# A two-layer decoder trunk: the order of TensorE's work around and inside the first layer's attention

## The chip, the cores and the metric

The kernel runs on one core of a Trainium2 chip. The core has TensorE (PE) for matrix products, VectorE (DVE), ScalarE (ACT) and GpSimd (POOL) for the rest, and SyncE (SP), which here only issues transfers. Each engine works through its own instructions in the order in which the program lists them, and semaphores hold it back until what it needs is there. The metric is the time of one execution on the device, in microseconds.

## The reference

Two layers on 512 positions of width 1024, each a token mixer and a feed-forward part, with a residual sum and a layer norm behind both. The change touches the mixer of the first layer, which is sixteen attention heads and an output projection:

```python
def even_mixer(x, w_in, w_uk, w_uv, b_f, w_o, rel_bias):
    h = x @ w_in
    q_a, c_kv, q_idx, k_idx, w_idx, q_b, k_b, v_b, f_in = _split(h, EVEN_WIDTHS)
    ...
    def block(args):                       # 128 queries at a time
        idx = jnp.einsum('bthd,bsd->bths', qi, k_idx)
        score = jnp.einsum('bth,bths->bts', wi, jax.nn.relu(idx)).astype(jnp.float32)
        score = jnp.where(causal[None], score, -jnp.inf)
        _, sel = lax.top_k(score, k_sel)   # 128 keys for each query
        ...
        la = jnp.einsum('bthr,btkr->bhtk', ql, c_sel).astype(jnp.float32)
        bias = rel_bias[t5_bucket(q_pos[None, :, None] - sel)]
        la = la + jnp.moveaxis(bias, -1, 1).astype(jnp.float32)
        ...
        oa = jnp.einsum('bhtk,btkr->bthr', pa, c_sel)
        lb = jnp.einsum('bthd,bshd->bhts', qb, k_b).astype(jnp.float32)
        lb = lb + jnp.swapaxes(fq, 1, 2)[..., None] - cum_f_keys[:, :, None, :]
        ...
        ob = jnp.einsum('bhts,bshd->bthd', pb, v_b)
    ...
    return jnp.concatenate([o_a, o_b], axis=-1) @ w_o
```

Eight heads "b" (first in the kernel, 0 to 7) attend with a forget bias to all earlier positions; eight heads "a" (8 to 15) attend to the 128 keys that the indexer's scores select, with a relative-position bias.

## The kernel before

Every large product is made from numbers split in two parts, high and low, and takes three products on TensorE: high by high, high by low and low by high (`mm3`, L175 to L177). A weight matrix comes by a transfer into `raw`, ScalarE casts its high part (L77), and VectorE, for some units GpSimd, makes the low part by subtraction (L81, L79). Units of the stream of weights are numbered in the order in which the program asks for them; units 10 to 17 are the projections of the "b" heads' pairs, 18 to 22 those of the "a" heads, 23 to 30 the output projection's.

The first layer's mixer runs in this order: the projections of the indexer's keys, the forget gates and the indexer's queries, the projection of c_kv; then the relative bias table (L418 to L437): a one-hot matrix and `rel_bias` are fetched, two small products (L422, L428) make the table, it is written to memory (`tb_d`), spread to one copy for each of 128 rows (`tp_d`), and read back shifted (`T5`), all transfers issued by GpSimd; then four transposes (L441) and the indexer's scores for the query blocks 1 to 3 (L457: for each of 8 indexer heads two products of 256, 384 or 512 columns; relu on ScalarE, L459; weighted sum on VectorE into `sel`, L462 and L464; masking on GpSimd, L466); then the values' projection of the "b" heads, and the projections of the first two pairs of heads.

After that the attention loop runs. For a head h it has four steps, which a string of letters, `SEQ`, orders: L makes the logits (for four query blocks 128, 256, 384 and 512 columns, three products each, over 64 rows of the array, into three banks); S is the softmax (VectorE adds the bias and takes the row's minimum, L616; ScalarE the exponential, L618); T transposes the weights, ten 128x128 blocks into one tile `tri` of three banks (L636), which ScalarE and VectorE then split into `pt` (L213, L214); V multiplies with the values (512, 384, 256 and 128 columns). B sets up the next head's bias, D divides by the sums, and a digit runs that many steps of `todo`, a generator of the projections that later heads need: filler for TensorE. One round does L of head h, T of head h-1 and V of head h-2:

```python
SEQ = "L2BT2SDV2"
```

The order on each engine isn't the source's: a scheduler simulates the program and places each instruction when it thinks that it can run. After the loop comes the output projection `out_ln`, its eight accumulators in eight banks, then the layer norm.

TensorE's results go to PSUM, which has eight banks. The kernel sets up three pools one after another: eight single banks up to the loop, five single ones and `tri` in the loop, eight single ones after it. A new pool opens a bank when the old pool's tiles in it are done with.

## Time and profile before

| | us |
|---|---|
| median of 3 runs | 1187.08 |
| lowest and highest run | 1183.45, 1188.37 |
| the profiled execution | 1182.65 |
| its span | 1180.9 |
| TensorE busy in it | 1158.8 |
| VectorE, ScalarE, GpSimd busy | 690.8, 465.5, 186.5 |

The profile is of one execution. Its span is the time from the first to the last instruction, and 1.75 us of the execution lie around it. A row of the time line has the start, the time for which the row was busy, the engine, the source line, the operation, what it writes and reads, and its shape; behind it, in brackets, the idle time of the engine just before and what ended it. Products are pipelined, so their recorded lengths overlap; what a product costs in a row is the distance of two starts.

### The profile page before, as it was taken

The page shows a single profiled execution, that of the slowest core. Times are in us where ns is not written, and L with a number is a line of the kernel's source. Part 1 is how long each engine was busy: PE and PEld are TensorE (multiplying, and loading weights), DVE is VectorE, ACT ScalarE, POOL GpSimd, SP SyncE. Part 2 cuts the span into 40 slices and gives each one's busy share as a digit, 9 for nine tenths or more (in the row PEclk, how much of TensorE's full clock was granted, in tenths as well). Part 3 has the DMA queues.
Part 4 walks back from the last instruction along what each step waited for, and adds up shares of the span by engine and source line. Part 5 has one row for each costly group of instructions (what it writes and reads, how often), then busy time and mean ns, then how long its engine had stood idle before and what let it go on. Part 6 is the DMA issues. An engine that isn't in the chain of part 4 may idle for free. (4 is left out here: it accounts for less than half of the span.)

```text
span 1180.9 us, 14445 instructions
## 1 busy us (share of the span) xinstructions
PE 1158.8 (98%) x5527; PEld 965.7 (82%) x5527; DVE 690.8 (59%) x1133; ACT 465.5 (39%) x703; POOL 186.5 (16%) x244
## 2 busy tenths in 40 slices
PE   8999999899999999999999999999999999999996
PEld 7787878688888888888888888889888888888885
DVE  6789865746665655652247854455666565652226
ACT  6615656722434444432134143332543434432121
POOL 1556654303000000010003200012000000010003
PEclk9999999999999999999999999999999999999999
DMA  6623202361223232343343234371223223344321
GB/s 236 204 94 105 66 19 64 115 216 72 72 91 106 89 107 89 113 141 118 128 152 117 80 100 132 118 239 72 89 90 100 97 91 105 107 143 143 97 81 72
DMA packets 41382, 132.03 MB, mean 112 GB/s; under 512 B 5448, under 2 KB 5520, under 8 KB 41312
## 3 DMA queue, kind: packets, MB, share of 16 engines
q1 hardware_dynamic: 36128, 115.36, 29.5%
q0 software_dynamic: 5056, 15.71, 4.3%
q8 instruction: 43, 0.70, 0.2%
q14 instruction: 27, 0.22, 0.1%
q10 hardware_dynamic: 128, 0.03, 0.0%
HBM read 122.63 MB, written 10.02 MB: 112 GB/s over the span
## 5 line engine op out<-in xcount | busy, mean ns | idle before, releaser
L175 PE MATMUL bank<-quad,whi 128*128 128x512 f32 (+2 forms) x932 | 355.2, 383 | 1.5 <-ACT whi L140 1.3
L177 PE MATMUL bank<-quad,wlo 128*128 128x512 f32 (+2 forms) x932 | 354.5, 380 | 0.0
L176 PE MATMUL bank<-quad,whi 128*128 128x512 f32 (+2 forms) x932 | 354.4, 380 | 0.0
L81 DVE TENSOR_TENSOR wlo<-raw,whi 128x1024 fp32r<-128x1024 f32 x149 | 182.6, 1225 | 282.7 <-ACT whi L77 281.9
L77 ACT CAST whi<-raw 128x1024 fp32r<-128x1024 f32 x159 | 167.5, 1053 | 258.2 <-PE bank L177 110.2
L175 PEld LDWEIGHTS bank<-quad,whi 128*128 128x128 f32 x932 | 175.7, 189 | 37.0 <-ACT whi L140 1.8
L177 PEld LDWEIGHTS bank<-quad,wlo 128*128 128x128 f32 x932 | 176.0, 189 | 32.5 <-issue 0.4
L176 PEld LDWEIGHTS bank<-quad,whi 128*128 128x128 f32 x932 | 176.2, 189 | 32.2
L175 PE MATMUL bank<-whi,quad 128*128 128x512 f32 x388 | 150.7, 390 | 1.2 <-ACT temp L667 1.2
L176 PE MATMUL bank<-wlo,quad 128*128 128x512 f32 x388 | 151.0, 389 | 0.0
L177 PE MATMUL bank<-whi,quad 128*128 128x512 f32 x388 | 150.8, 389 | 0.0
L232 POOL DMA_DIRECT2D temp<-x x24 | 13.1, 548 | 568.1 <-ACT quadx L343 424.6
L175 PE MATMUL bank<-quad 128*128 128x512 f32 (+5 forms) x280 | 99.9, 361 | 1.9 <-DVE quad L214 1.4
L176 PE MATMUL bank<-quad 128*128 128x512 f32 (+5 forms) x280 | 98.3, 352 | 0.6 <-DVE quad L81 0.6
L177 PE MATMUL bank<-quad 128*128 128x512 f32 (+5 forms) x280 | 97.7, 350 | 0.0
L175 PEld LDWEIGHTS bank<-whi,quad 128*128 128x128 f32 x388 | 72.8, 188 | 16.4 <-ACT temp L667 1.3
L177 PEld LDWEIGHTS bank<-whi,quad 128*128 128x128 f32 x388 | 72.8, 188 | 15.2
L176 PEld LDWEIGHTS bank<-wlo,quad 128*128 128x128 f32 x388 | 72.9, 188 | 14.8
L312 DVE SCALAR_TENSOR_TENSOR temp<-bank,fcw,temp 128x511 f32<-128x511 f32 x88 | 65.5, 744 | 9.1 <-ACT temp L311 9.1
L314 DVE SCALAR_TENSOR_TENSOR temp<-bank,fcw,temp 128x510 f32<-128x510 f32 x88 | 65.9, 749 | 3.0
L175 PEld LDWEIGHTS bank<-quad 128*128 128x128 f32 (+1 forms) x280 | 52.3, 188 | 14.6 <-issue 3.2
L311 ACT ACTIVATE temp<-bank,fcw 128x512 f32<-128x512 f32 x88 | 60.0, 681 | 10.8 <-PE bank L177 10.8
(156 smaller groups left out, 1251.2 us busy)
## 6 DMA issues: line engine op xcount, KB each, us to landing
raw<-in_ws_dram SPq DMA_DIRECT2D x190, 512.0 KB, 3.5
x<-temp SPq DMA_DIRECT2D x24, 256.0 KB, 2.0
temp<-x POOLq DMA_DIRECT2D x24, 256.0 KB, 3.2
temp<-in_xT_dram SPq DMA_DIRECT2D x8, 256.0 KB, 5.8
temp<-fk_d SPq DMA_DIRECT2D x8, 256.0 KB, 6.6
temp<-rd_d SPq DMA_DIRECT2D x16, 128.0 KB, 3.1
temp<-in_x_dram POOLq DMA_DIRECT2D x8, 256.0 KB, 3.5
quad<-in_ln_g_dram POOLq DMA_DIRECT2D x4, 512.0 KB, 5.9
```

Source lines behind the costliest of these rows:

```text
L77: nc.scalar.copy(hi, t)
L81: dve[0] = nc.vector.tensor_tensor(out=lo, in0=t, in1=_f(hi), op=ALU.subtract)
L175: nc.tensor.matmul(out, a[0], b[0], start=first, stop=False)
L176: nc.tensor.matmul(out, a[0], b[1], start=False, stop=False)
L177: return nc.tensor.matmul(out, a[1], b[0], start=False, stop=last)
L232: nc.gpsimd.dma_start(t, src[n * 128:n * 128 + 128, hf * 512:hf * 512 + 512])
L311: nc.scalar.mul(t, p, cw[:, j, 2:3])
L312: nc.vector.scalar_tensor_tensor(out=t[:, 1:], in0=p[:, :S - 1], scalar=cw[:, j, 1:2], in1=t[:, 1:], op0=ALU.mult, op1=ALU.add)
L314: nc.vector.scalar_tensor_tensor(out=t[:, 2:], in0=p[:, :S - 2], scalar=cw[:, j, 0:1], in1=t[:, 2:], op0=ALU.mult, op1=ALU.add)
```

## The change

Five things change together.

- **Banks.** Five banks are set up for the whole kernel, and three more for `tri` up to the end of the attention; afterwards these three are single banks as well, and `bank()` takes from the five or the three by turns. Nothing is closed in front of the loop. What comes before the attention now has five banks and not eight.
- **Bias table.** It stands behind the indexer's scores in the source, and the transposes and scores in front of it.
- **Turns.** The filler steps are single products (`mms`) and not triples; `turn` puts one behind each of its ten transposes; the logits and the values take a short and a long block by turns (`both`): 128 with 384 and 256 with 512 in the logits, 512 with 128 in the values. `SEQ` has 4, 2 and 3 steps, which with the ten makes 19 products a round; before it was 6 triples.
- **Output projection.** `begin` makes its first half, the part over heads 0 to 7, as a generator: eight accumulators of 12 products each. From round 15 on it is the filler; what is left runs in `out_ln`. The weights' units 26 to 32 go into tiles of another pool (`quad`).
- **Order.** In the attention loop TensorE's instructions stay in the order of the source (`manual_schedule`); the other engines' order is still the scheduler's.

```diff
-SEQ = "L2BT2SDV2"
+SEQ = "L4BT2SDV3"
...
-    psum = ExitStack()
-    ps = [psum.enter_context(tc.tile_pool(name="ps", bufs=8, space=PSUM))]
+    ps5 = E(tc.tile_pool(name="ps5", bufs=5, space=PSUM))
+    ps3 = ExitStack()
+    tri = ps3.enter_context(tc.tile_pool(name="tri", bufs=1, space=PSUM))
+    more = []
+    turnus = [0]
 
     def bank():
-        return ps[0].tile([128, 512], F32, name="bank")
+        turnus[0] += 1
+        pool = more[0] if more and turnus[0] % 8 >= 5 else ps5
+        return pool.tile([128, 512], F32, name="bank")
 
     def temp():
         return tmp.tile([128, 512], F32, name="temp")
...
+    def mms(out, a, b, first, last):
+
+        for i, (u, v) in enumerate(((a[0], b[0]), (a[0], b[1]), (a[1], b[0]))):
+            nc.tensor.matmul(out, u, v, start=first and i == 0, stop=last and i == 2)
+            yield
+
+    def both(*runs):
+
+        runs = list(runs)
+        while runs:
+            for r in list(runs):
+                if next(r, "end") == "end":
+                    runs.remove(r)
...
         for n in range(NCH):
             rs.append(load_res(res_src, n))
+            while begun is not None and pb[min(n + 1, NCH - 1)][1] is None and next(run, "end") != "end":
+                pass
...
+        for j in (1, 2, 3):
+            scores(j)
 
         oh = temp()
         nc.gpsimd.dma_start(oh[:32], A["onehot"])
...
-        for j in (1, 2, 3):
-            scores(j)
         bg = choose()
...
-            for j in range(NCH):
+
+            def run(j):
                 n = 128 * (j + 1)
                 c = slice(j * 128, j * 128 + 128)
-                mm3(lg[j], (q[r, 0, c], q[r, 1, c]), (q[r, 2, :n], q[r, 3, :n]), True, True)
+                return mms(lg[j], (q[r, 0, c], q[r, 1, c]), (q[r, 2, :n], q[r, 3, :n]), True, True)
+
+            both(run(0), run(2))
+            both(run(1), run(3))
...
                     nc.tensor.transpose(p[:, o:o + 128], d[:, OFF[j] + i * 128:OFF[j] + i * 128 + 128], ident)
+                    fill(1)
...
-            for k in range(NCH):
+
+            def run(k):
                 f = slice(64 * hv - b0, 64 * hv + 64)
                 c = slice(PO[k], PO[k] + 512 - 128 * k)
-                mm3(p[:m, k * 128:], (v[0][:, k, f], v[1][:, k, f]), (pt[:, 0, c], pt[:, 1, c]), k == 0, k == NCH - 1)
+                return mms(p[:m, k * 128:], (v[0][:, k, f], v[1][:, k, f]), (pt[:, 0, c], pt[:, 1, c]),
+                           k == 0, k == 2)
+
+            both(run(0), run(3))
+            both(run(1))
+            both(run(2))
...
+        def begin():
+
+            us = [unit() for _ in range(4)]
+            for n in range(NCH):
+                for hf in range(2):
+                    p = bank()
+                    for k in range(4):
+                        yield from mms(p, lhs(k, n), wk(us[k], hf * 512, hf * 512 + 512), k == 0, False)
+                    pb[n][hf] = p
+
+        begun = begin()
+        for k in range(26, 33):
+            ws.big[k] = quad
...
-        psum.close()
-        ps[0] = psum.enter_context(tc.tile_pool(name="psh", bufs=5, space=PSUM))
-        tri = psum.enter_context(tc.tile_pool(name="tri", bufs=1, space=PSUM))
         bias(0)
+        hold = ExitStack()
+        hold.enter_context(tc.manual_schedule(engines={mybir.EngineType.PE}))
         for h in range(20):
             for c in SEQ:
                 if c == "L" and h < 16:
                     while h // 2 not in finished and next(todo, "end") != "end":
                         pass
                     logits(h)
+                    if h == 15:
+                        for _ in todo:
+                            pass
+                        todo = begun
...
-        psum.close()
-        ps[0] = psum.enter_context(tc.tile_pool(name="psm", bufs=8, space=PSUM))
...
+        hold.close()
+        ps3.close()
+        more.append(ps3.enter_context(tc.tile_pool(name="ps3", bufs=3, space=PSUM)))
...
-        xt, late = out_ln(lhs, 8, A["x"], 0, 0, x1, 2)
+        xt, late = out_ln(lhs, 8, A["x"], 0, 0, x1, 2, begun=(pb, begun))
```

Three places in the order of the instructions, before and after. The first is GpSimd's order from the splits of the weights of the values' projection on (before, with the fetch of the one-hot matrix in front of them):

```order
L418 DMA temp_385<-in_onehot_dram 32x512
L394 DMA fk_d_229<-temp_213 8x512
L79 TENSOR_TENSOR wlo_584<-raw_581,whi_583 128x1024
L79 TENSOR_TENSOR wlo_590<-raw_587,whi_589 128x1024
L79 TENSOR_TENSOR wlo_761<-raw_758,whi_760 128x1024
L426 DMA tb_d_393<-temp_391 8x384
L432 DMA tp_d_399<-tb_d_393 1024x1x384
L466 AFFINE_SELECT sel1_415<-sel1_415 128x128
L466 AFFINE_SELECT sel2_416<-sel2_416 128x128
L434 DMA T5_401<-tp_d_399 128x8x256
L466 AFFINE_SELECT sel3_417<-sel3_417 128x128
```

After:

```order
L417 DMA fk_d_232<-temp_216 8x512
L79 TENSOR_TENSOR wlo_587<-raw_584,whi_586 128x1024
L79 TENSOR_TENSOR wlo_593<-raw_590,whi_592 128x1024
L79 TENSOR_TENSOR wlo_764<-raw_761,whi_763 128x1024
L466 AFFINE_SELECT sel1_397<-sel1_397 128x128
L488 DMA temp_553<-in_onehot_dram 32x512
L466 AFFINE_SELECT sel2_398<-sel2_398 128x128
L496 DMA tb_d_561<-temp_559 8x384
L466 AFFINE_SELECT sel3_399<-sel3_399 128x128
L502 DMA tp_d_567<-tb_d_561 1024x1x384
L504 DMA T5_569<-tp_d_567 128x8x256
```

The fetch has moved from the front to behind the masking of the first score matrix, and the table's three other transfers stand behind it. The same place on TensorE, from the last two products of the indexer's scores, before:

```order
L457 MATMUL bank_556<-quad_78,quad_231 128x512 x2
L457 MATMUL bank_562<-quad_78,quad_232 128x512 x2
L175 MATMUL bank_595<-quad_322,quad_79 128x512
L176 MATMUL bank_595<-quad_322,quad_79 128x512
L177 MATMUL bank_595<-quad_322,quad_81 128x512
```

After:

```order
L457 MATMUL bank_538<-quad_81,quad_234 128x512 x2
L457 MATMUL bank_544<-quad_81,quad_235 128x512 x2
L492 MATMUL bank_557<-temp_553,rb_555 8x384
L498 MATMUL bank_563<-rb_555,temp_553 128x8
L180 MATMUL bank_598<-quad_325,quad_82 128x512
L181 MATMUL bank_598<-quad_325,quad_82 128x512
```

The two small products, which stood in front of the transposes and scores before (L422, L428), now stand between the scores and the first product of the values' projection; `temp_553` is the one-hot matrix.

The second place is VectorE in the rounds of heads 12 and 13: `d` is a head's logits with the bias, `bank` TensorE's logits, `pt` the split transposed weights, and `wlo`/`quad` with `raw` a low part of weights. Before, from the last pass over the logits of head 12 (`d_2112`) to the last one over those of head 13 (`d_2190`):

```order
L616 ISA d_2112,mn_2215<-bank_2175,d_2112 128x512
L616 ISA mn_2215 128x1
L682 TENSOR_TENSOR quad_2062<-temp_2064,quad_2062 128x512
L214 TENSOR_TENSOR pt_2212<-tri_2197,pt_2212 128x1280
L616 ISA d_2190,mn_2281<-bank_2245,d_2190 128x128
L616 ISA mn_2281 128x1
L616 ISA d_2190,mn_2281<-bank_2245,d_2190 128x256
L616 ISA mn_2281 128x1
L626 RECIPROCAL rd_2225<-den_2216 128x4
L616 ISA d_2190,mn_2281<-bank_2246,d_2190 128x384
L616 ISA mn_2281 128x1
L616 ISA d_2190,mn_2281<-bank_2247,d_2190 128x512
```

After, up to the same last pass (`d_2188`) and the row behind it:

```order
L81 TENSOR_TENSOR quad_2401<-raw_2399,quad_2401 128x1024
L81 TENSOR_TENSOR quad_2406<-raw_2404,quad_2406 128x1024
L643 ISA d_2188,mn_2279<-bank_2244,d_2188 128x384
L643 ISA mn_2279 128x1
L81 TENSOR_TENSOR quad_2411<-raw_2409,quad_2411 128x1024
L643 ISA d_2188,mn_2279<-bank_2243,d_2188 128x128
L643 ISA mn_2279 128x1
L643 ISA d_2188,mn_2279<-bank_2243,d_2188 128x256
L643 ISA mn_2279 128x1
L643 ISA d_2188,mn_2279<-bank_2245,d_2188 128x512
L643 ISA mn_2279 128x1
L232 TENSOR_TENSOR pt_2210<-tri_2195,pt_2210 128x1280
```

The subtraction that frees `tri` of head 11 (`pt_2212` before, `pt_2210` after) stood in front of the passes over head 13's logits, and stands behind them now, with three splits of the output projection's weights ahead of it; `mn` is the row minimum that each pass leaves.

The third place is TensorE at the transposes of head 15, the last ones, before (`pt` with `quad_1547` are values' products):

```order
L175 MATMUL bank_2420<-pt_2346,quad_1547 128x128
L176 MATMUL bank_2420<-pt_2346,quad_1547 128x128
L177 MATMUL bank_2420<-pt_2346,quad_1548 128x128
L175 MATMUL bank_2458<-pt_2406,quad_1547 64x512
L636 MATMUL tri_2437<-ident_134,d_2324 128x128 x10
L638 MATMUL tri_2437<-ident_134,rd_2359 8x128
L176 MATMUL bank_2458<-pt_2406,quad_1547 64x512
L177 MATMUL bank_2458<-pt_2406,quad_1548 64x512
L175 MATMUL bank_2458<-pt_2406,quad_1547 64x384
```

After:

```order
L663 MATMUL tri_2481<-ident_137,d_2322 128x128
L187 MATMUL bank_2437<-quad_2401,quad_1697 128x512
L663 MATMUL tri_2481<-ident_137,d_2322 128x128
L187 MATMUL bank_2485<-whi_1862,quad_1212 128x512
L663 MATMUL tri_2481<-ident_137,d_2322 128x128
L187 MATMUL bank_2485<-wlo_1863,quad_1212 128x512
L663 MATMUL tri_2481<-ident_137,d_2322 128x128
L187 MATMUL bank_2485<-whi_1862,quad_1212 128x512
L663 MATMUL tri_2481<-ident_137,d_2322 128x128
L187 MATMUL bank_2485<-whi_1979,quad_1212 128x512
L663 MATMUL tri_2481<-ident_137,d_2322 128x128
L187 MATMUL bank_2485<-wlo_1980,quad_1212 128x512
```

Products of the output projection (`whi`, `wlo` with `quad_1212`, which holds heads 0 to 3) stand between the transposes, where there was nothing.

## Rows read from the trace of the kernel before

**Rows 1.** The page: TensorE's busy time; its granted clock in tenths.

```profile
PE 1158.8 (98%) x5527; PEld 965.7 (82%) x5527; DVE 690.8 (59%) x1133; ACT 465.5 (39%) x703; POOL 186.5 (16%) x244
...
PEclk9999999999999999999999999999999999999999
```

**Rows 2.** Busy time (and instructions) by stretch, then granted clock, DMA share, GB/s.

```profile
7.00:13.00 6.00, 5.80 (x15) 5.05 (x16) 5.44 (x8) 5.11 (x9) 1.03 (x2) 1.00 1.04 390
13.00:20.00 7.00, 7.00 (x36) 6.27 (x35) 2.61 (x4) 2.51 (x3) 0.00 (x0) 1.00 0.68 239
93.00:205.00 112.00, 110.60 (x606) 88.95 (x605) 82.24 (x212) 68.72 (x153) 61.01 (x93) 1.00 0.21 66
222.00:237.00 15.00, 10.05 (x63) 7.91 (x61) 9.50 (x11) 9.87 (x17) 2.15 (x4) 1.00 0.53 161
```

**Rows 3.** Time line of TensorE around the scores: start, busy time, engine, line.

```profile
37.61 0.81 PE L422 MATMUL bank<-temp,rb 32*8 32x384 f32 x2
...
38.66 0.66 PE L441 MATMUL bank<-ident,temp 128*128 128x128 f32 x4
...
42.10 7.66 PE L457 MATMUL bank<-quad 128*128 128x256 f32 x40 [1.82 <-ACT far L430]
49.60 0.39 PE L175 MATMUL bank<-quad 128*128 128x512 f32 x1
```

**Rows 4.** Time line of TensorE, first product of the first head.

```profile
94.68 0.32 PE L175 MATMUL bank<-quad 64*128 64x128 f32 x1 [1.40 <-DVE quad L214]
```

**Rows 5.** Time line of TensorE, end of the attention.

```profile
231.63 0.50 PE L175 MATMUL bank<-pt,quad 128*128 128x512 f32 x1 [1.61 <-ACT pt L213]
...
236.20 0.50 PE L175 MATMUL bank<-whi,quad 128*128 128x512 f32 x1 [1.16 <-ACT temp L667]
```

**Rows 6.** Time line of TensorE, a block of logits cut in two.

```profile
210.81 0.39 PE L177 MATMUL bank<-quad 64*128 64x512 f32 x1
211.13 0.51 PE L175 MATMUL bank<-pt,quad 128*128 128x512 f32 x1
211.57 0.33 PE L175 MATMUL bank<-quad 64*128 64x128 f32 x1
```

**Rows 7.** Time line of TensorE, transposes and what follows.

```profile
104.72 1.25 PE L636 MATMUL tri<-ident,d 128*128 128x128 f32 x10
105.72 0.48 PE L175 MATMUL bank<-quad 128*128 128x512 f32 x1
106.04 0.39 PE L176 MATMUL bank<-quad 128*128 128x512 f32 x1
```

**Rows 8.** Time line of VectorE, the last eleven accumulations of the scores.

```profile
49.91 7.51 DVE L464 SCALAR_TENSOR_TENSOR sel<-temp,wi,sel 128x384 f32<-128x384 f32 x11
```

**Rows 9.** Time line of ScalarE, in front of the scores' relus.

```profile
41.58 0.47 ACT L424 ACTIVATE temp<-bank 8x384 f32<-8x384 f32 x1
```

**Rows 10.** Time line of GpSimd, the masking of the scores.

```profile
49.14 6.02 POOL L466 TENSOR_SCALAR_AFFINE_SELECT sel<-sel 128x128 f32<-128x128 f32 x2 [0.31 <-DVE sel L464]
...
61.07 0.30 POOL L466 TENSOR_SCALAR_AFFINE_SELECT sel<-sel 128x128 f32<-128x128 f32 x1
```

**Rows 11.** Transfers: issues, KB each, median us from issue to landing.

```profile
tp_d<-tb_d POOLq DMA_DIRECT2D x1, 1536.0 KB, 11.8
...
temp<-in_onehot_dram POOLq DMA_DIRECT2D x1, 64.0 KB, 4.2
```

**Rows 12.** Time line of VectorE in the attention's last heads.

```profile
205.50 1.22 DVE L81 TENSOR_TENSOR wlo<-raw,whi 128x1024 fp32r<-128x1024 f32 x1
...
209.24 1.49 DVE L214 TENSOR_TENSOR pt<-tri,pt 128x1280 fp32r<-128x1280 f32 x1 [0.23 <-ACT pt L213]
...
211.73 0.69 DVE L616 CUSTOM_DVE_ANT_0 d<-bank,d 128x512 f32<-128x512 f32 x1
```

**Rows 13.** Time line of TensorE in the first microseconds.

```profile
8.11 0.63 PE L177 MATMUL bank<-quad,wlo 128*128 128x512 f32 x1
8.54 0.52 PE L176 MATMUL bank<-quad,whi 128*128 128x384 f32 x1
```

More of the change, by code (lines that the diff above doesn't have):

```diff
@@ L196, in proj_steps @@
         for k in range(8):
-            mm3(p, wk(w, k * 128, k * 128 + 128), xk(xt, k), k == 0, k == 7)
-            yield
+            yield from mms(p, wk(w, k * 128, k * 128 + 128), xk(xt, k), k == 0, k == 7)
     last_mm = [None]
@@ L269, in ln_turn, with out_ln @@
             cut2(xt[0][hf][:, :, c], xt[1][hf][:, :, c], p.rearrange("p (a b) -> p a b", a=4))
-    def out_ln(lhs, nk, res_src, l, i, dst, nbig, last=False):
-        pb = [[None, None] for _ in range(NCH)]
-        for hf in range(2):
-            for n in range(NCH):
-                pb[n][hf] = bank()
+    def out_ln(lhs, nk, res_src, l, i, dst, nbig, last=False, begun=None):
         head = nk - TAIL
-        for k in range(head, nk + (0 if last else nbig)):
-            ws.big[base[0] + k] = quad
-        for k in range(head):
-            w = unit()
+        if begun is None:
+            pb = [[None, None] for _ in range(NCH)]
             for hf in range(2):
                 for n in range(NCH):
-                    mm3(pb[n][hf], lhs(k, n), wk(w, hf * 512, hf * 512 + 512), k == 0, False)
+                    pb[n][hf] = bank()
+            for k in range(head, nk + (0 if last else nbig)):
+                ws.big[base[0] + k] = quad
+            for k in range(head):
+                w = unit()
+                for hf in range(2):
+                    for n in range(NCH):
+                        mm3(pb[n][hf], lhs(k, n), wk(w, hf * 512, hf * 512 + 512), k == 0, False)
+        else:
+            pb, run = begun
         us = [unit() for _ in range(TAIL)]
@@ L688, in work, with lhs @@
                 yield from pair_a(i)
+        def lhs(k, n):
+            c = slice(n * 128, n * 128 + 128)
+            return oq[k // 2][:, k % 2, c], oq[k // 2][:, 2 + k % 2, c]
+        pb = [[None, None] for _ in range(NCH)]
+        def begin():
+            us = [unit() for _ in range(4)]
+            for n in range(NCH):
+                for hf in range(2):
+                    p = bank()
+                    for k in range(4):
[4 more added lines that the diff above has]
+            ws.big[k] = quad
         for i in range(2):
@@ L723, in _body @@
                     fill(int(c))
-        psum.close()
-        ps[0] = psum.enter_context(tc.tile_pool(name="psm", bufs=8, space=PSUM))
-        def lhs(k, n):
-            c = slice(n * 128, n * 128 + 128)
-            return oq[k // 2][:, k % 2, c], oq[k // 2][:, 2 + k % 2, c]
+        hold.close()
+        ps3.close()
+        more.append(ps3.enter_context(tc.tile_pool(name="ps3", bufs=3, space=PSUM)))
         fcw = [None, None]
```

43 lines of the change are left out of this document (21 added, 22 removed).

## The prediction

> **What bounds the kernel now.** I read the busy times first. TensorE is busy 1158.8 of 1180.9 us and its clock is at full level in nearly every slice [rows 1], so only two things can move the time: the products' own cost, and the idle time between them, about 22 us in all. The order listing shows as many products of the same shapes after the change as before, so the first is open only where a product's cost depends on its neighbours. The second I read by stage and then wait by wait. In the attention's long part, 93 to 205 us, TensorE is busy 110.60 of 112.00 us [rows 2]: nothing to win there, only to lose. The idle time that the change can touch lies at three places: in front of the indexer's scores (1.82 us), at the first head (1.40 us) and at the end of the attention (4.95 us) [rows 2, 3, 4].
>
> **Base.** The sum is made against the profiled execution, 1182.65 us. The three other times shown run from 1183.45 to 1188.37 with a median of 1187.08, so the profiled one lies 4.4 us under the median. The mean of the four is 1185.4, and I add the sum to that, since the traces don't tell which of the four is typical.
>
> **Banks set up once.** Before, a first head waits 1.40 us while VectorE empties the old banks, since the new set cannot open before the old one is empty [rows 4]. After, the same five banks stay, and the head finds free ones: **-1.4 us**. The scores now have five banks instead of eight. Before, TensorE gets through eight products there and then waits for ScalarE [rows 3]; with five banks it stops earlier and starts again at the same moment, because ScalarE's first relu sets that moment. I cost it at nothing; it would cost if the relus were slower than the products, and 7.66 us for 40 products with the relus keeping pace says they are not.
>
> **Output projection begun within the attention.** Between 222 and 237 us TensorE is busy 10.05 of 15.00 us, so 4.95 are idle, in waits of up to 1.61 us on the cast and the subtraction of the transposed weights, and the last, 1.16 us, on the copy ahead of the projection [rows 2, 5]. In the new order the transposes of heads 14 and 15 and the last three rounds have 65 products of the projection between them, at 0.23 us each 15 us of work that waits for nothing in those heads (it reads heads 0 to 7). I take all of the idle time as covered: **-4.9 us**, at least -3 if the last wait, for the output of head 15, stays. The weights' splits that this needs are moved ahead, and are costed below.
>
> **Logits in one piece.** The logits use 64 rows of the array, all else 128. Each crossing costs time: a lone 128-row product between two logits blocks takes 211.13 - 210.81 = 0.32 us to begin and 0.44 us until the next starts, 0.76 for two steps that take 0.23 each in a row [rows 6], so a block cut in two costs 0.30 us. The order listing of before has four such cuts, in the last heads; after has none: 4 x 0.30 = **-1.2 us**.
>
> **Short products by turns with long ones.** Ten transposes and the start of the product behind them take 106.04 - 104.72 = 1.32 us, with 0.23 for that product's own step 0.109 each [rows 7]. A transpose of 128 columns has half the columns of a 256 product, which steps at 0.12, so 0.06 would be its own streaming; the rest is the load of its weights, and the weights of the *next* product load while it runs. The long product behind the last transpose steps at 106.04 - 105.72 = 0.32 us and not 0.23: the 0.09 that it lacks is that load, which a short neighbour can't cover. So I expect a short one to cost its 0.11 wherever it stands: **0 us**. The other end: if a long neighbour hides the load, 120 of the 160 transposes (those with filler between them) win 0.05 each, 6.0 us, and the 48 logits of 128 columns as much each, 2.4 us: -8.4 us. Nothing in the rows makes it cost, beyond one such 0.09 per pair that I count as the transpose's own. The Trainium skill, TensorE: Matmul & The Clock Gate, section "Back-to-back issue gap", gives 81 ns for a stream of loads and products of 128 columns; by that figure, as an estimate, the 120 transposes would win 0.03 us each, 3.4 us, and the sum below would come out at 1186.5. The row shows 109 ns for the same thing, and the row decides.
>
> **The bias table behind the scores.** This is the largest term. Before, the one-hot matrix is fetched at the start, long ahead, and its products stand in front of the transposes and scores [rows 3]. After, the fetch (L488) writes into a slot of the temporaries that the scores use, so it waits for VectorE to finish the fourth of the last eleven accumulations (that of the third 512-wide score); and on GpSimd it stands behind the masking of the first score matrix. TensorE's order puts the two small products right behind the scores and in front of the value projection (L180 after), and TensorE works in order, so the whole projection waits for the fetch. In numbers: eleven accumulations take 7.51 us from 49.91 [rows 8], so the fourth ends at 49.91 + 4 x 0.68 = 52.6. The scores start about 0.4 us sooner, as ScalarE's scaling of 0.47 us (L424) no longer stands in front of the relus [rows 9]: 52.2. The masking: two take 6.02 us from 49.14, and a single one elsewhere 0.30 [rows 10], so the first seems to take 5.7, until 54.9, less 0.4: 54.5. The fetch is issued between 52.2 and 54.5, and lands 4.2 us after [rows 11]: 56.4 to 58.7. From the first of the two small products to the transposes it took 38.66 - 37.61 = 1.05 us [rows 3]; the two follow the landing, so the value projection starts at 57.4 to 59.8 where it started at 49.60 [rows 3]: +7.8 to +10.2. I take the middle, **+9.0 us**, since a GpSimd span of 5.7 us that is 0.30 elsewhere may be a record's and not the instruction's. Nothing gives it back: TensorE is busy without a break afterwards, and work that is ahead elsewhere doesn't shorten its queue. The rest of the table (11.8 us for the broadcast, its largest transfer [rows 11]) ends some 25 us later, about 80, ahead of the first head at 94.7 [rows 4]: no cost.
>
> **TensorE's order is the source's.** In heads 10 to 13 the fillers from the projections have run out (19 a head now, 18 before), and the transposes stand bare behind the next head's logits. One of these waits is plain in the order of VectorE: three splits of the projection's weights come early, and the subtraction that frees the transposes' banks for head 12 stands behind all of head 13's logits. From the last logits product, the 512-wide pass of 0.69 us and the subtraction of 1.49 us follow [rows 12]: at least 2.2 us in which TensorE has nothing. If the split of 1.22 us [rows 12] and the two short passes (0.3 and 0.4) also fall behind the logits, it is 4.1. I take **+3.0 us**; the lower end is 0, if the splits' data come late and the subtraction gets ahead in time.
>
> **Sum.** -1.4 - 4.9 - 1.2 + 0 + 9.0 + 3.0 = +4.5 us, and 1185.4 + 4.5 = **1189.9 us**, 0.2% over the median shown.
>
> **Rivals.**
> *The loads are hidden (0.22).* Then 8.4 us come off: 1181.5, and the lower end of the bias term would make it 1180. For it: the change gives every short product a long neighbour, whose 0.23 us is longer than a load. Against it: the 0.32 us step behind the last transpose [rows 7]. The Trainium skill, TensorE: Matmul & The Clock Gate, section "Step-by-step: what each phase is for", says that a load of the next weights may run during the present product; that is what the 0.23 us steps with changing weights show too, and it leaves open whether the load behind a short product can start still earlier.
> *The clock falls in the wait (0.16).* Slower. TensorE stands idle for 8 to 10 us behind the scores, longer than anywhere in the trace of before after its start. In the first microseconds a product of 512 columns steps at 8.54 - 8.11 = 0.43 us, twice the later 0.23, which is the 1.2 GHz level (though the window's granted clock already reads 1.00), and up to 13 us it stays so: 15 products in 6 us against 36 in the next 7 [rows 2, 13]. If the wait brings the engine back there for as long, 5.8 us of work goes at half rate and 2.9 us are lost: 1192.8. It decides itself by the length of the wait: no row tells which length does it, the waits of 1 to 2 us in the trace don't. The Trainium skill, same page, section "HAM oscillation — how this bites in real kernels", says that a wait for a transfer can throw the engine back to half rate each time; no run here shows it yet.
> *The order of the source waits in every bare head (0.10).* Slower. If the subtraction falls behind the logits in each of heads 10 to 13, 4 x 2.2 = 8.8 us stand for the 3.0: 1195.7. Against it: in the heads without splits the new order of VectorE has the subtraction in front of the logits' passes.
> *The waits are shorter than I count (0.10).* The fetch at its early end (-1.2) and no wait in head 12 (-3.0): 1185.7; with half of the bias term hidden it is 1181. That the change doesn't do what it says is ruled out by the order: the 65 products do stand between the transposes.
>
> **How the numbers follow.** My forecast has 0.42. The measurement can tell about 0.5% from no change, 5.9 us: below 1181.1 is faster, above 1193.0 slower. Of the forecast's 0.42, about 0.30 lies within and 0.12 above (clock apart, both large terms at their upper ends give 1192.2 and a little more in other heads passes the line). Hidden loads: 0.16 faster, 0.06 within. Clock: 0.13 slower, 0.03 within. Bare heads: 0.10 slower. Shorter waits: 0.09 faster or just within, of which I give 0.08 to faster and 0.02 to within. Together faster 0.24, same 0.41, slower 0.35. The range goes from 1179 (hidden loads at the early fetch) to 1197 (the clock with both terms at their upper ends, 1189.9 + 1.2 + 1.1 + 2.9 = 1195.1, and the bare heads at 1195.7).
>
> **What would show it.** In the trace of after: a wait of TensorE of 7 to 11 us behind the last score, ended by the fetch of the one-hot matrix; the granted clock of the products behind it; no wait at the first head; less than 2 us of idle time from the transposes of head 14 to the projection; pairs of transpose and long product that step at 0.34 us together (0.28 would mean hidden loads); one wait of 2 to 4 us in front of the transposes of head 12. I am wrong if the fetch is issued before the scores end, if a pair takes 0.28, or if waits of a microsecond appear in the heads that have filler.

## The result, and the profile after

| | before | after |
|---|---|---|
| median, us (10 runs each) | 1187.09 | 1193.65 |
| lowest and highest | 1183.45, 1191.78 | 1189.0, 1194.92 |
| span of the profiled execution | 1180.9 | 1187.3 |
| TensorE busy in it | 1158.8 | 1162.2 |

The changed kernel is slower: ratio 1.0054, 95% interval 1.0037 to 1.0072, which is 6.4 us. The forecast was 1189.9 us in a range of 1179 to 1197. The profiled execution of the changed kernel took 1189.0 us and is the fastest of its ten; the other nine lie between 1191.9 and 1194.9 us.

The longest waits of TensorE after the change (time in total, times, longest):

```profile
PE tri L663 <- DVE pt L232: 5.1, 1, 5.1
PE bank L492 <- DMA temp<-in_onehot_dram: 2.8, 1, 2.8
PE bank L457 <- DVE quad L432: 2.0, 1, 2.0
PE bank L457 <- ACT wi L446: 1.8, 1, 1.8
```

Two of them are the ones forecast: the transposes of head 12 wait for the subtraction that frees their banks, and the bias table's products wait for the one-hot matrix, though for 2.8 us here and not for the 7 to 11 forecast. The wait at the first head [rows 4] is gone. Around the scores the time line of TensorE, which answers to [rows 3], has:

```profile
38.31 0.47 PE L457 MATMUL bank<-quad 128*128 128x256 f32 x2 [2.00 <-DVE quad L432]
40.56 10.51 PE L457 MATMUL bank<-quad 128*128 128x256 f32 x42 [1.77 <-ACT wi L446]
53.88 1.43 PE L492 MATMUL bank<-temp,rb 32*8 32x384 f32 x2 [2.81 <-DMA temp<-in_onehot_dram]
...
55.77 0.80 PE L180 MATMUL bank<-quad 128*128 128x512 f32 x1
...
59.77 0.48 PE L180 MATMUL bank<-quad 128*128 128x512 f32 x1
```

42 score products take 10.51 us where 40 took 7.66 before, and nine products of the value projection take 59.77 - 55.77 = 4.00 us where nine steps of 0.23 are 2.1. Stretches of the changed kernel show why (their length, busy time and products of TensorE and of the others, then the granted clock):

```profile
40.00:46.00 6.00, 5.44 (x20) 5.45 (x21) 4.89 (x9) 5.03 (x15) 2.15 (x1) 0.50 0.58 186
...
47.00:53.00 6.00, 4.07 (x19) 3.06 (x17) 5.49 (x11) 4.93 (x11) 0.83 (x2) 1.00 0.02 5
...
54.00:59.00 5.00, 5.00 (x12) 3.06 (x11) 2.15 (x3) 0.66 (x2) 0.84 (x2) 0.50 0.61 211
...
221.00:227.00 6.00, 3.23 (x13) 3.07 (x14) 2.87 (x10) 3.07 (x10) 1.20 (x3) 0.50 0.71 221
```

The clock is at 0.50, the lower of its two levels (1.2 of 2.4 GHz), in three stretches, each just behind or inside one of the waits above; in the profiled execution of before it is at full level in the same places. So a wait has two prices, its own and that of the slow products behind it.

At the end of the attention nothing is left of the 4.95 us [rows 2, 5] (the same columns as above):

```profile
226.00:240.00 14.00, 14.00 (x84) 11.48 (x83) 8.08 (x22) 8.76 (x22) 4.89 (x9) 0.96 0.26 77
240.00:262.00 22.00, 22.00 (x115) 18.14 (x114) 10.47 (x10) 9.39 (x12) 3.47 (x7) 1.00 0.54 166
```

TensorE is busy without a gap from 226 to 262 us, in which the last transposes, the last values and the start of the projection lie. That part of the change does what it says; its price lies earlier, in front of head 12 (TensorE, then VectorE):

```profile
223.77 2.39 PE L663 MATMUL tri<-ident,d 128*128 128x128 f32 x10 [5.08 <-DVE pt L232]
```

```profile
216.33 2.89 DVE L81 TENSOR_TENSOR quad<-raw,quad 128x1024 fp32r<-128x1024 f32 x2
219.14 0.54 DVE L643 CUSTOM_DVE_ANT_0 d<-bank,d 128x384 f32<-128x384 f32 x1
...
219.62 1.53 DVE L81 TENSOR_TENSOR quad<-raw,quad 128x1024 fp32r<-128x1024 f32 x1
...
221.63 0.68 DVE L643 CUSTOM_DVE_ANT_0 d<-bank,d 128x512 f32<-128x512 f32 x1
...
222.24 1.48 DVE L232 TENSOR_TENSOR pt<-tri,pt 128x1280 fp32r<-128x1280 f32 x1
```

The three splits take 4.4 us of VectorE in the middle of a round without filler, and the subtraction into `pt` ends at 223.7, when the transposes start.

The pairs of a transpose and a long product:

```profile
236.86 0.27 PE L663 MATMUL tri<-ident,d 128*128 128x128 f32 x1
236.89 0.49 PE L187 MATMUL bank<-wlo,quad 128*128 128x512 f32 x1
237.21 0.27 PE L663 MATMUL tri<-ident,d 128*128 128x128 f32 x1
237.24 0.48 PE L187 MATMUL bank<-whi,quad 128*128 128x512 f32 x1
```

A pair steps at 237.21 - 236.86 = 0.35 us. With 0.23 for the long product, 0.12 is left for the transpose, as much as it costs in a row (0.11 [rows 7]): the long neighbour hides nothing that can be seen.

### The profile page after: what moved, and what is told of

Same layout as the page of the kernel before. It is cut to its first block, busy times and chain, and to the rows that moved or that the text cites. A ratio compares the mean times of both kernels' runs of the same rounds, so it can differ in the third digit from the quotient of the medians.

```text
span 1187.3 us, 14425 instructions
## 1 busy us (share of the span) xinstructions
PE 1162.2 (98%) x5527; PEld 966.4 (81%) x5527; DVE 694.8 (59%) x1133; ACT 465.7 (39%) x703; POOL 186.5 (16%) x244
## 5 line engine op out<-in xcount | busy, mean ns | idle before, releaser
L180 PE MATMUL bank<-quad,whi 128*128 128x512 f32 (+2 forms) x860 | 324.9, 379 | 1.8 <-ACT whi L145 1.4
L181 PE MATMUL bank<-quad,whi 128*128 128x512 f32 (+2 forms) x860 | 325.3, 378 | 0.0
L182 PE MATMUL bank<-quad,wlo 128*128 128x512 f32 (+2 forms) x860 | 325.2, 378 | 0.0
L180 PEld LDWEIGHTS bank<-quad,whi 128*128 128x128 f32 x860 | 161.5, 188 | 32.4 <-ACT whi L145 1.7
L181 PEld LDWEIGHTS bank<-quad,whi 128*128 128x128 f32 x860 | 161.7, 188 | 29.7 <-DVE quad L153 0.2
L182 PEld LDWEIGHTS bank<-quad,wlo 128*128 128x128 f32 x860 | 161.7, 188 | 29.5
L181 PE MATMUL bank<-wlo,quad 128*128 128x512 f32 x356 | 138.5, 389 | 0.0
L182 PE MATMUL bank<-whi,quad 128*128 128x512 f32 x356 | 138.4, 389 | 0.0
L180 PE MATMUL bank<-whi,quad 128*128 128x512 f32 x356 | 138.3, 390 | 0.0
L180 PEld LDWEIGHTS bank<-whi,quad 128*128 128x128 f32 x356 | 66.8, 188 | 14.0
L181 PEld LDWEIGHTS bank<-wlo,quad 128*128 128x128 f32 x356 | 66.8, 188 | 13.9
L182 PEld LDWEIGHTS bank<-whi,quad 128*128 128x128 f32 x356 | 66.8, 188 | 13.8
L181 PE MATMUL bank<-quad 128*128 128x512 f32 (+1 forms) x192 | 69.2, 362 | 0.7 <-DVE quad L81 0.6
L180 PE MATMUL bank<-quad 128*128 128x512 f32 (+1 forms) x192 | 68.8, 363 | 0.5 <-ACT quad L231 0.5
L182 PE MATMUL bank<-quad 128*128 128x512 f32 (+1 forms) x192 | 68.5, 358 | 0.0
L187 PE MATMUL bank<-quad 128*128 128x512 f32 (+4 forms) x288 | 65.2, 364 | 0.9 <-DVE quad L235 0.9
```

Of the source, the lines that this page charges most:

```text
L180: nc.tensor.matmul(out, a[0], b[0], start=first, stop=False)
L181: nc.tensor.matmul(out, a[0], b[1], start=False, stop=False)
L182: return nc.tensor.matmul(out, a[1], b[0], start=False, stop=last)
L187: nc.tensor.matmul(out, u, v, start=first and i == 0, stop=last and i == 2)
```

## The experiments

Each kernel is the changed kernel or one built on it. Ratios are to the kernel before.

| kernel | what | median, us | ratio | 95% interval |
|---|---|---|---|---|
| after | | 1193.65 | 1.0054 | 1.0037 to 1.0072 |
| e1_table_front | table ahead of the scores | 1184.06 | 0.9976 | 0.9959 to 0.9992 |
| e2_onehot_early | fetch early, products behind | 1185.1 | 0.9988 | 0.9972 to 1.0004 |
| e3_splits_late | splits of three units later | 1194.53 | 1.0063 | 1.0041 to 1.0085 |
| e4_no_turns | no turns | 1192.45 | 1.0048 | 1.003 to 1.0065 |
| e5_spread | e1, filler spread | 1179.92 | 0.9944 | 0.9926 to 0.9962 |
| e6_no_begun | e1, projection not begun | 1179.24 | 0.994 | 0.9924 to 0.9957 |
| e8_eight_banks | e1, eight banks ahead | 1182.23 | 0.9968 | 0.9955 to 0.9981 |
| e9_scheduled | e1, scheduler's order | 1181.14 | 0.9943 | 0.9922 to 0.9965 |
| e10_spread_no_begun | e5 and e6 | 1183.99 | 0.998 | 0.9963 to 0.9996 |
| e11_spread_eight_late | e5, e8 and e3 | 1179.5 | 0.9941 | 0.9919 to 0.9963 |
| e12_no_begun_eight | e6 and e8 | 1178.35 | 0.992 | 0.9898 to 0.9942 |

**The table back in front.**

```diff
+        oh = temp()
+        nc.gpsimd.dma_start(oh[:32], A["onehot"])
...
         p = bank()
         for n in range(NCH):
             nc.tensor.transpose(p[:, n * 128:n * 128 + 128], cw[:, n * 128:n * 128 + 128], ident)
```

> The changed kernel with the relative bias table put back in front of the transposes and the scores; all else as changed. Theory A (the table's place costs): the wait for the one-hot fetch (2.8 us) goes, TensorE enters the scores later and waits once, about 2 us as before, so that the clock falls neither at 40 nor at 53 us; the value projection's tenth product starts near 51.7 us and not at 59.8. About 8 us less than the changed kernel: 1185.5, ratio to the kernel before 0.998 to 1.000. Theory B (the five banks in front of the attention are to blame for the fall of the clock in the scores): the fall at 40 us stays and some 4.8 us are won: 1189, ratio 1.0015.

Measured 0.9976, against 1.0054 for the changed kernel: the table's place costs 0.8%, some 9 us. The value projection starts at 51.58 us at full clock (its tenth product at 53.6, not at 51.7). But one detail of theory A fell: the clock still goes to 0.50 behind the scores' wait, at 42 us. With the table in front the kernel is already 0.24% faster than before.

**The one-hot matrix early, the products behind.**

```diff
+        T5 = mc.tile([128, NH, 256], F32)
+        nc.gpsimd.dma_start(T5[:32, 0:2, :].rearrange("p a b -> p (a b)"), A["onehot"])
...
-        oh = temp()
-        nc.gpsimd.dma_start(oh[:32], A["onehot"])
+        oh = T5[:, 0:2, :].rearrange("p a b -> p (a b)")
```

> The changed kernel with the one-hot matrix fetched in front of the transposes, into the (later overwritten) table tile, so that no temporary is needed; its two small products stay behind the scores. Theory A: TensorE finds the matrix there behind the scores: 2.8 us of wait and the second fall of the clock (about 3.2 us) go, the first fall at 40 us stays: 1187.5, ratio 1.0005. If the second fall were not tied to that wait, only 2.8 us go: 1191, ratio 1.003. The difference to the kernel with the table in front is then the price of the first fall with its longer wait, 2 us or more.

Measured 0.9988: the late fetch is the loss, not the place of the products. The two kernels' intervals overlap, so no price of the first fall can be read from their difference.

**The splits later.**

```diff
+        m = nc.scalar.copy(hi, t)
+        if i in self.late:
+            self.tc.add_manual_dep(m.ins, dve[0].ins.name, AFTER, reason="not ahead of the attention's own")
```

> The changed kernel with the casts of the output projection's units 26 to 28 tied behind VectorE's work at the place in the source, so that the subtraction which frees the transposes' banks of head 11 stands ahead of the last pass over head 13's logits again. Theory A: the 5.1 us in front of the transposes of head 12 shrink to at most 1 us, and the clock doesn't fall at 221 us (3 us): about 7 us less than the changed kernel, 1186.6, ratio 0.9995. Theory B (TensorE's fixed order is to blame, not the splits): the wait turns up at head 13 or 14 in the same size, 1193, ratio 1.005.

Measured 1.0063, the same as the changed kernel: theory B's time. Part of the wait moved one round on (TensorE, heads 12 and 13):

```profile
224.82 2.40 PE L668 MATMUL tri<-ident,d 128*128 128x128 f32 x10 [1.32 <-DVE pt L237]
...
234.34 1.79 PE L668 MATMUL tri<-ident,d 128*128 128x128 f32 x10 [2.62 <-DVE pt L237]
```

1.32 + 2.62 = 3.9 us for 5.08. The wait of 1.32 us still has one split in front of the subtraction. In front of the second one VectorE isn't busy with splits: the last of the three ends at 228.7 us, and VectorE then stands idle until the logits of head 14 come (VectorE, e3):

```profile
230.81 0.56 DVE L648 CUSTOM_DVE_ANT_0 d<-bank,d 128x384 f32<-128x384 f32 x1 [2.10 <-PE bank L192]
...
232.71 1.49 DVE L237 TENSOR_TENSOR pt<-tri,pt 128x1280 fp32r<-128x1280 f32 x1
```

The subtraction into `pt` stands behind the four passes over those logits in VectorE's order, although ScalarE's half of `pt` is done at 229.2. So the place of the subtraction alone costs 2.62 us in a round without filler; the splits ahead of it make the wait longer.

**No turns.**

```diff
-            both(run(0), run(2))
-            both(run(1), run(3))
+            for j in range(NCH):
+                both(run(j))
...
-                    fill(1)
+            fill(10)
```

> The changed kernel without turns: the logits and values one block after the other from short to long (values from long to short), the ten filler products behind the ten transposes and not between them; the same products otherwise. Theory A (a short product costs its own load of weights wherever it stands): the same time as the changed kernel within 1.5 us, 1193.6, ratio 1.0054. Theory B (a long neighbour hides the load): up to 8 us slower, 1202, ratio 1.012.

Measured 1.0048, the same. Theory A stands, as the pairs of 0.35 us say too. This kernel's profile (and e3's) also shows the other way in which the table's wait comes about. GpSimd in the changed kernel, then in this one, and TensorE's wait in this one:

```profile
48.10 0.29 POOL L466 TENSOR_SCALAR_AFFINE_SELECT sel<-sel 128x128 f32<-128x128 f32 x1 [5.94 <-DVE sel L464]
51.70 0.53 POOL L488 DMA_DIRECT2D temp<-in_onehot_dram  x1 [3.32 <-DVE sel L464]
```

```profile
49.66 5.25 POOL L466 TENSOR_SCALAR_AFFINE_SELECT sel<-sel 128x128 f32<-128x128 f32 x1 [5.92 <-DVE sel L464]
54.86 0.53 POOL L488 DMA_DIRECT2D temp<-in_onehot_dram  x1
```

```profile
PE bank L492 <- DMA temp<-in_onehot_dram: 8.6, 1, 8.6
```

In one execution the masking takes 0.29 us, the fetch is issued at 51.70 when VectorE has freed its slot, lands 2 us later, and TensorE waits 2.8 us; in the other the masking takes 5.25, the fetch is issued at 54.86, lands 4.4 us later, and the wait is 8.6 us. In the second the clock didn't fall in the scores but at 54 us, inside the long wait, and stayed low to 64 us, with 4.9 us of products in that time. The clock, and longer waits within the scores, take back a part of the 5.8 us between the two waits, not all of it: from the transposes to the first logits it is 66.3 us in the first execution and 68.7 in the second (the table further down). The first also came there 2.4 us sooner, because around 8 us its products of 512 columns step at 0.23 us already and those of the second at 0.42. In all, the executions took 1189.0 and 1193.4 us. Since the changed kernel's other nine runs lie at 1191.9 to 1194.9 us, and e3's profiled execution, with a wait of 8.3 us, at 1194.6, the long wait is probably the usual one; no trace of a second execution of the changed kernel shows it.

**Filler spread.** Built on e1, as the rest is.

```diff
-                    fill(1)
+                    fill((i + j) % 2)
```

> The kernel with the table in front (e1_table_front), and with four fillers between the transposes and not ten, so that a round has 13 products of filler and the projections last to round 13; only the transposes of head 13 stand bare. Theory A (the early splits cost 5.2 us plus a fall of the clock in head 12 because nothing else stands there for TensorE): the wait in front of head 12's transposes goes below 1 us and the clock doesn't fall near 216 us: 7 us under e1_table_front, 1177, ratio 0.992. Theory B (rounds with less filler wait more everywhere, VectorE being the bound of a round): waits of 0.5 us or more in the early heads, and the sum stays at 1184, ratio 0.998.

Measured 0.9944: 0.3% less than e1, with intervals that just touch. The wait of 5.1 us is gone. Smaller ones of 0.5 and 0.8 us have come to head 13 instead (0.3 us of the first row lies earlier, at 200 us), where the last pair's projection is now finished just in time, with a fall of the clock behind them (217 to 224 us). The three splits come one at a time here, between 204 and 212 us, so this run changes their place together with the filler. The waits of head 13:

```profile
PE bank L187 <- DVE quad L235: 1.1, 2, 0.8
PE bank L187 <- ACT quad L234: 0.5, 1, 0.5
```

**The projection not begun.**

```diff
-                    if h == 15:
-                        for _ in todo:
-                            pass
-                        todo = begun
...
-        xt, late = out_ln(lhs, 8, A["x"], 0, 0, x1, 2, begun=(pb, begun))
+        xt, late = out_ln(lhs, 8, A["x"], 0, 0, x1, 2)
```

> The kernel with the table in front (e1_table_front), without the output projection begun in the attention: no filler from round 15 on, the weights' units in their usual tiles and time. Theory A: the wait of 5.2 us in head 12 and the clock's fall there (3 us) go, since no splits come early, and the waits at the end of the attention (about 5 us in the kernel before) come back, perhaps with a fall of the clock of their own: between -4 and +1 us of e1_table_front, 1182.5, ratio 0.996. Theory B (the wait in head 12 comes of TensorE's fixed order): it stays, and the time is 5 us over e1_table_front: 1189, ratio 1.002.

Measured 0.994. Without the projection in the attention the kernel is 0.36% faster than with it. In head 12 nothing waits; at the end two waits come back, 2.4 of the 4.95 us before, and the clock doesn't fall there:

```profile
PE bank L187 <- ACT pt L231: 1.5, 1, 1.5
PE tri L663 <- DVE pt L232: 0.9, 1, 0.9
```

**Eight banks ahead of the attention.**

```diff
-    tri = ps3.enter_context(tc.tile_pool(name="tri", bufs=1, space=PSUM))
-    more = []
+    more = [ps3.enter_context(tc.tile_pool(name="ps3a", bufs=3, space=PSUM))]
...
+        more.clear()
+        ps3.close()
+        tri = ps3.enter_context(tc.tile_pool(name="tri", bufs=1, space=PSUM))
         bias(0)
```

> The kernel with the table in front (e1_table_front), and with eight banks in front of the attention as before (five for the whole kernel, three more that are given up for the transposes' tile in front of the loop). Theory A (the five banks do not set the moment at which the scores go on): the same as e1_table_front within 1 us, 1184, ratio 0.9975, with one more wait of up to 1 us at the first transposes. Theory B (five banks stop TensorE earlier, which makes the wait in the scores long enough for the clock to fall at 42 us): no fall there, 1.5 to 2 us less, 1182, ratio 0.996.

Measured 0.9968 against 0.9976, with intervals that overlap: theory A as far as can be told. The clock falls at 42 us as in e1.

**The kernel before, once more.**

> The kernel before, once more, to see another execution of it: the profiled one was 4.4 us under the median. If the median is due to the clock of TensorE falling in the scores in most executions, this one is near 1187 us and the granted clock is at 0.5 for some microseconds behind 42 us. If it is again near 1183 us the clock is at full level all along, as in the first.

One execution: 1186.96 us, and the clock is at 0.50 in three places where the first profile had it at full level (behind the scores' wait, behind the first head's wait, and in the tail):

```profile
43.00:45.00 2.00, 2.00 (x9) 2.00 (x9) 1.35 (x3) 1.68 (x6) 0.80 (x2) 0.50 0.56 190
98.00:103.00 5.00, 5.00 (x13) 3.48 (x12) 4.43 (x15) 2.83 (x9) 1.69 (x1) 0.50 0.43 149
237.50:239.50 2.00, 1.89 (x5) 1.70 (x6) 0.05 (x1) 0.37 (x1) 0.54 (x1) 0.50 0.45 174
```

Same kernel, nearly the same waits, 4.3 us more. The execution profiled first was one in which none of these waits cost the clock. The wait at the first head is 1.40 us in both, so its length alone doesn't decide.

**The scheduler's order again.**

```diff
-        hold.enter_context(tc.manual_schedule(engines={mybir.EngineType.PE}))
```

> The kernel with the table in front (e1_table_front), with TensorE's order in the attention left to the scheduler as before; turns, begun projection and single banks as changed. Theory A (the fixed order does no harm of its own; the early splits do): the wait in front of head 12's transposes shrinks or moves, since the scheduler knows of the splits and puts other products there if there are any; without any filler left it stays: 1184 within 3 us, ratio 0.9975. Theory B (the fixed order makes the waits): the wait of 5 us and the clock's fall go and nothing else changes: 1176, ratio 0.991.

Measured 0.9943, 0.33% less than e1 (the intervals overlap a little) and between the two expectations (0.9975 and 0.991). The wait of 5.1 us in head 12 is not there; one of 1.0 us is left in the round of head 13's logits, and one of 0.7 us ahead of the output projection:

```profile
214.49 0.56 PE L187 MATMUL bank<-pt,quad 128*128 128x512 f32 x2 [1.00 <-ACT pt L231]
...
256.07 0.50 PE L187 MATMUL bank<-whi,quad 128*128 128x512 f32 x1 [0.67 <-ACT temp L701]
```

The three splits still stand on VectorE between 211 and 217 us. So the early splits alone don't make the wait: with an order that the scheduler fits to them, a fifth of it is left. The clock still falls there, from 215 to 222 us.

**Combinations.** e10 is the edits of e5 and e6 together, e11 those of e5, e8 and e3, e12 those of e6 and e8.

> The kernel with the table in front, 13 products of filler in a round (e5_spread) and no begun output projection (e6_no_begun). Each of the two alone gave 1179.5. If both only cure the same wait in head 12, together they give the same, 1179.5, ratio 0.994. If they cure different waits (the spread filler also covers the heads 11 to 14 that run bare in e6_no_begun), 2 to 3 us less: 1177, ratio 0.992.

Measured 0.998, worse than either alone. Its waits are those of both, 1.4 and 0.9 us in the tail and 0.8 and 0.5 us at head 13: the spread filler creates waits of its own, with the clock low behind them from 219 to 226 us, and has no wait in head 12 to cure.

> The kernel with the table in front, 13 products of filler in a round, the output projection begun, eight banks in front of the attention, and the splits of units 26 to 28 tied behind VectorE's work at their place in the source: the changed kernel with the two places mended where it waits. Compared with e5_spread (1179.9) the waits of 0.7 and 1.0 us at head 13's logits and the clock's fall there (217 to 224 us) should go: 1175, ratio 0.9905. If the late splits only move the wait, as in e3_splits_late, 1180, ratio 0.9945.

Measured 0.9941, no better than e5: the late splits and the eight banks gain nothing here. The waits at head 13's logits are still there, 0.5 and 0.8 us, as in e5; the expectation's 0.7 and 1.0 us were misread.

> e6_no_begun with eight banks in front of the attention. In e6_no_begun the scores wait 0.5 and 2.1 us and the clock falls behind them; with eight banks the first wait was 0.3 and the clock fell all the same (e8_eight_banks). So the same as e6_no_begun within 1 us: 1178.5, ratio 0.9935; 1176 (0.991) if the clock holds in most executions.

Measured 0.992 (0.9898 to 0.9942), the lowest of all and faster than both kernels of the case; from e6 it can't be told apart.

To compare executions in which different waits fell to the clock, the spans cut at three points of TensorE's time line (start of the table or transposes ahead of the scores; first logits; first transposes of the layer norm), in us:

| | to the scores | to the first logits | to the layer norm | to the end |
|---|---|---|---|---|
| before | 37.6 | 57.1 | 178.2 | 908.1 |
| before, once more | 36.8 | 59.2 | 182.1 | 907.2 |
| after | 35.2 | 66.3 | 178.0 | 907.8 |
| e4_no_turns | 37.6 | 68.7 | 177.0 | 908.3 |
| e1_table_front | 36.8 | 58.4 | 179.9 | 908.0 |
| e6_no_begun | 37.9 | 58.2 | 174.9 | 906.7 |
| e12_no_begun_eight | 36.5 | 59.3 | 174.9 | 906.1 |

The second column holds the table: 7 to 12 us over before where it stands behind the scores. The third holds the attention and the projection. With the projection begun early it is 177.0 to 179.9 us, at most 1.2 us less than in the first profile of before; the second one needs 3.9 us more there, with the clock low for some 10 us of it (97 to 104 and 237 to 240 us). Without the projection begun early it is 174.9.

## Why the prediction came out as it did

The direction was right, and the time lay within the range. The change was larger than the sum: +6.4 us against +4.5. Of the 3.7 us between 1189.9 and the median of 1193.65, 1.7 are the base (1185.4 for a median of 1187.09); the table's place took 9.3 us (1.0054 against 0.9976) where 9.0 stood, and all other terms together gave -2.8 us (e1) where -4.5 stood. Point by point:

- **The bias table, +9.0 us.** Undoing it gave 9.3 us. The bounds had two possible moments of the fetch, with the masking at 0.3 or at 5.7 us; both occur, in different executions, and the long masking is not only a record's length: in e3 and e4 the fetch is issued right behind it. The wait of 7 to 11 us that was to be seen is there in those two (8.3 and 8.6 us) and not in the profile of the changed kernel (2.81). "Nothing gives it back" left out the clock, which adds slow products behind either wait. That the middle of the two bounds comes so close to the measured 9.3 is in part luck.
- **Head 12, +3.0 us.** The mechanism was right, the size too small: 5.08 us of wait. Behind the last logits product stand not one split of 1.22 us but the end of the second, the third of 1.53 us, and all four passes, ahead of the subtraction of 1.48 us. Then 3.23 us of products ran at half rate behind the wait, which costs about another 1.6. I named the subtraction's place and the early splits as the cause. e3 shows the place alone, one round on, at 2.62 us, near the lower end of 2.2; without begun projection and its splits (e6) nothing waits in head 12; with other products there for TensorE (e5, e9) the wait of 5 us goes although the splits come early. How much of e5 is the filler and how much the splits that come one at a time is open.
- **The end of the attention, -4.9 us.** Gone, as forecast. But e6 gets half of it (two waits of 2.4 us in all are left) without begun products, and the begun projection costs more than it gains: +0.36% with it.
- **The first head, -1.4 us.** No wait there any more.
- **Turns, 0.** 0.35 us a pair (0.34 forecast), and no difference without them (e4). The rival of the hidden loads (0.22) falls. The Trainium skill, TensorE: Matmul & The Clock Gate, section "Back-to-back issue gap", would have given 81 ns for a short product; the runs show 0.11 to 0.12 us.
- **The scores with five banks, 0.** With eight banks the time is the same within the intervals. This was tried with the table in front only. The waits of the changed kernel's profile differ for another reason: TensorE got there 2.4 us sooner (35.2 against 37.6 us) and waited for the indexer's last queries instead. The change doesn't make it sooner (e4: 37.6 us); in this execution the products of the first microseconds step at 0.23 us, where those of before step at 0.43 [rows 13].
- **The clock, a rival with 0.16.** It happened, and not in one place but three. My step "the waits of 1 to 2 us in the trace don't" do it failed: it was true of one execution only. The kernel before, profiled once more, has the clock at 0.50 behind those same waits, at nearly the median's time; that would explain why the base was 4.4 us under the median. The rival's step "decides itself by the length of the wait" failed as well: 1.40 us at the first head did it in one execution and not in the other. The rival's price was 2.9 us for one fall behind the long wait. Behind the table's wait the changed kernel's profile lost 1.9 us (4.00 for 2.1), and in the scores about 2.6 (42 products in 10.51 us for 40 in 7.66, less 0.24 for two more of 256 columns).
- **Not foreseen.** The wait of 0.7 us of TensorE in the second layer (L803 before) is not there after the change. Whether the banks taken by turns do that was not tried. A wait of 0.9 us of the logits is new (at 196 us, for VectorE's part of the last pair's projection); in e1 the clock falls behind it, from 192.5 to 196 us. The prediction had waits of a microsecond in the heads with filler among its signs of being wrong.

What stays open: the logits in one piece (-1.2 us) were not tried alone, and the difference of e1 to e9 holds that term, the fixed order and the head-12 wait at once.

## What to carry to other kernels

A step that is moved in the source takes its transfers along: look at which buffer the transfer writes and what must be free before it can be issued, and fetch early whatever needs nothing. Filler that is begun early isn't free when its weights must be prepared by engines that the rounds without other filler are waiting for. And with TensorE at 98%, a wait of 2 us can cost as much again and more in slow products behind it: removing small waits can pay more than their sum. One profile of a kernel does not tell which of them cost the clock, and it may be of an unusual execution: look where its time lies among the other runs, on both sides of the comparison.

## What the runs showed of the hardware

- TensorE's granted clock falls to half inside or behind waits of about 1 to 8.6 us, and the same wait of the same kernel may or may not do it: the 1.82 us at the scores [rows 3] and the 1.40 us at the first head [rows 4] did not in the first profile of before, 1.97 and 1.40 us at the same places did in the second. It stayed low for 3 to 10 us at a time.
- In the first microseconds the granted clock of a row can read 1.00 while products of 512 columns step at 0.43 us, the lower level (before, 7.7 to 13 us). The same stretch runs at 0.23 us a product in the changed kernel's profile, which is worth about 2.4 us between two executions.
- The masking of the first score matrix on GpSimd takes 0.29 to 0.61 us or 5.2 to 5.8, at the same place of the program in fourteen profiles, nothing in between (seven of each). In all long ones it ends within 0.2 us of the first 0.1 us gap in VectorE's row of sums. The Trainium skill, SBUF — State Buffer, section "Who interferes with whom", says that the two engines share a pair of ports as an exclusive lock. That fits the long ones; some short ones also began while VectorE ran without a gap, which it doesn't explain, and no run here tested it.
